# A two-layer hybrid decoder trunk on one core: the fifth Strassen product gets its own PSUM bank, and the turned tiles land in 1 KB rows

## The chip, the cores and the metric

The kernel runs on one core of one Trainium2 chip. The metric is the device time of one execution in microseconds (us), the median of three runs. Lower is better.

## The reference, cut to what matters

Two layers work on 256 rows of 2048 channels, all in float32. Each layer normalises its input, multiplies it with one wide weight matrix (`w_in`, 7680 columns), runs sliding-window attention and a spatial gating unit on parts of the product, projects both branches, merges them with sigmoid gates, multiplies with `w_out`, and adds the residual. Then comes a SwiGLU block with 5632 hidden channels.

```
for l in range(DEPTH):                       # DEPTH = 2, x: (1, 256, 2048) float32
    h = rms_norm(x, mix_norm[l])
    q, k, v, uv, gate_logits = jnp.split(h @ w_in[l], cuts, axis=-1)
...
    branch_a = sliding_window_attention(q, k, v, sinks[l]) @ w_attn_branch[l]
    branch_b = chunked_sgu(jax.nn.gelu(uv), w_spatial[l], b_spatial[l],
                           sgu_ln_g[l], sgu_ln_b[l]) @ w_sgu_branch[l]
    gates = jax.nn.sigmoid(gate_logits)
    merged = gates[..., :D_MODEL] * branch_a + gates[..., D_MODEL:] * branch_b
    x = x + merged @ w_out[l]
    h2 = rms_norm(x, ffn_norm[l])
    x = x + (jax.nn.silu(h2 @ w_gate[l]) * (h2 @ w_up[l])) @ w_down[l]
```

## The kernel before, in words

Everything is a list of **jobs**. A job multiplies the 256 rows with 1024 columns of a weight matrix (two column halves, c = 0 and c = 1, of 512 each; t = 0 and t = 1 are the two halves of the rows). The inner dimension is cut into **units** of 512 channels. To keep float32 accuracy each operand is split into a high part and a low part that TensorE (PE) takes as `fp32r`, and each product is three matmuls, `three` (L343 to L346): high by high, high by low, low by high.

A weight tile of 256 channels by 512 columns is a **part**. For each part SyncE loads raw weights (`raw`, four buffers of 1 MB), ScalarE (ACT) rounds them into `whi` (L224, six buffers), and VectorE (DVE) subtracts to get `wlo` (L232, five buffers). `Stream.fill` prepares parts some five ahead of PE: `whi` of part n + 6 and `wlo` of part n + 5 can be written once PE is done with part n.

In a "whole" step PE does 12 matmuls: one part with the two row halves. In 42 of the jobs (those with `m=1`, here called Strassen jobs) the first unit is done by Winograd's form of Strassen's algorithm instead: seven products of six matmuls each in place of four whole steps. The products are called 11, t1, t2, 22, t3, 21, t4; four of them need sums of weights, which DVE makes (L216, tiles `sum` and `raw`), and sums of the activations (`sh`, `sl`). The sum for t4 is the last of these four. The accumulators are PSUM banks a, e, x, y, four out of five; the fifth is idle in such a job. After product 11 ACT copies bank a into x (L383); after t1 it copies bank e, the fifth product, to SBUF (`p5`, the tile that the profile calls p; L385 and L369); after t2 it copies a to SBUF (`u2`, tile u, L387); after t3 it copies a into y (L389). PE's next product on the same bank has to wait for the copy: 22 is added into e, so it waits for p; t3 is added into a, so it waits for u; t4 is added into y. After t4 DVE adds u into e (L391) and p into a (L392). Banks x and y are C11 and C12 (column half 0), e and a are C21 and C22 (column half 1). Then the other units follow as whole steps, first both halves of column half 0, then both of column half 1 (L131 to L134).

Evictions are queued by `evicting` (L275). Column half 0 is done two steps before the job ends. For column half 1 row half 0 is evicted at once, row half 1 and a follow-up `then` are put off: time is counted in slots, a whole step is one slot, a Strassen product half a slot; behind a job whose successor is a Strassen job they come `T1_LATE` = 3 and `THEN_LATE` = 4 slots later.

The follow-up turns a result of 256 rows by 512 channels into the next job's stationary operand (`transposed`, L476). DVE transposes blocks of 32 by 32 (`blk`, L438, two instructions), GpSimd (POOL) issues 16 DMAs of 32 KB from SBUF to SBUF (`gathered`, L443), each in rows of 32 elements at the destination, into the tile `tt`. Then ACT rounds `tt` to `uh` (L486) and DVE makes `ul` (L493) one slot later. The place at which these readers are queued is reckoned from `G_BUSY` = 3.5 and `G_LAND` = 1.5 slots. An up-projection of the SwiGLU block, `w_out`, the second branch, and the last `w_down` have such a follow-up; for the second branch it begins with a merge of two gate tiles (L1003).

The order on every engine is that of the program as it is written; each engine works through its own list and waits where data is missing.

Of the kernel before, what the change touches and what calls it, by code (L numbers as in the profile page):

```python
# [14 lines left out]
P = 128  # L15
# [22 lines left out]
G_BUSY, G_LAND = 3.5, 1.5  # L38
T1_LATE, THEN_LATE = 3, 4
# [11 lines left out]
def hybrid_trunk(ctx: ExitStack, tc: tile.TileContext, x, mix_norm, w_in, q_norm, k_norm, sinks,  # L51
# [37 lines left out]
    PRODUCTS = ("11", "t1", "t2", "22", "t3", "21", "t4")  # L89
# [18 lines left out]
    def add_job(cols, units=None, m=0):  # L108
# [239 lines left out]
    def run(units, done):  # L348
# [3 lines left out]
        held = {}  # L352
# [13 lines left out]

        def kept(name, src):
            held[name] = temp(name=name)
            nc.scalar.activation(held[name], src, AF.Copy)  # L369

        for n, (name, u, at) in enumerate(job.steps):
# [3 lines left out]
            if name != "whole":  # L375
# [5 lines left out]
                if at:  # L381
                    if name == "11":
                        nc.scalar.activation(x, a, AF.Copy)  # L383
                    elif name == "t1":
                        kept("p5", e)  # L385
                    elif name == "t2":
                        kept("u2", a)  # L387
                    elif name == "t3":
                        nc.scalar.activation(y, a, AF.Copy)  # L389
                    elif name == "t4":  # L390
                        nc.vector.tensor_tensor(out=e, in0=e, in1=held["u2"], op=ALU.add)  # L391
                        nc.vector.tensor_tensor(out=a, in0=a, in1=held["p5"], op=ALU.add)  # L392
# [41 lines left out]
    def gathered(dst, src):  # L434
# [5 lines left out]
        ov = dst.rearrange("p k (t i c) -> p i (k t) c", t=NT, c=B)  # L440
        for i in range(4):
            for j in range(4):
                nc.gpsimd.dma_start(ov[j * B:(j + 1) * B, i],  # L443
                                  blk[i * B:(i + 1) * B, j].rearrange("p k t c -> p (k t) c"))
        gather_end[0] = max(gather_end[0], slot_no[0]) + G_BUSY
        return gather_end[0] + G_LAND - slot_no[0]

    def combine(unit, f, n, then=None):

        s4 = slot([P, 4, 2, P], name="sums")  # L450
        a11, a12, a21, a22 = (f[:, 2 * h:2 * h + 2, t * P:(t + 1) * P] for t in range(2) for h in range(2))

        def low(hi, lo, full):
            nc.vector.tensor_tensor(out=flat(lo), in0=flat(full), in1=flat(hi.bitcast(F32)), op=ALU.subtract)

        def first():
            for i, (p, q, op) in enumerate(((a21, a22, ALU.add), (s4[:, 0], a11, ALU.subtract),
                                            (a11, a21, ALU.subtract), (a12, s4[:, 1], ALU.subtract))):
                nc.vector.tensor_tensor(out=s4[:, i], in0=p, in1=q, op=op)
            if then is not None:  # L460
                nc.scalar.activation(unit.hi, f, AF.Copy)

        def second():
            if then is not None:
                low(unit.hi, unit.lo, f)
            nc.scalar.activation(unit.shi, s4, AF.Copy)

        def third():
            low(unit.shi, unit.slo, s4)
# [6 lines left out]
    def transposed(units, c, src, scale=None, cols=None, on_pe=False, sums=False, at_once=False):  # L476
# [3 lines left out]
        def scaled(k):  # L480
            return (scale or 1.0) if cols is None else cols[:, k:k + 1]
# [40 lines left out]
        tt = slot([P, 4, S], name="tt")  # L522
        n = gathered(tt, src)
        if not sums:
            after(n, lambda: highs(0, 4, tt))
            after(n + 1, lambda: (lows(0, 2, tt[:, 0:2]), lows(2, 2, tt[:, 2:4]), ready()))
            return

        def scale_all():
            if cols is not None or scale is not None:  # L530
                for k in range(4) if cols is not None else (None,):
                    kk = slice(0, 4) if k is None else slice(k, k + 1)
                    nc.scalar.activation(tt[:, kk], tt[:, kk], AF.Copy, scale=scaled(k))

        after(n, scale_all)
        combine(unit, tt, n + 1, ready)

    class Norm:
# [7 lines left out]
        def add_sums(self, c):  # L546
# [5 lines left out]
            combine(unit, f, 1)  # L552
# [49 lines left out]
    nc.gpsimd.dma_start(cs, cosine.rearrange("(t p) h -> p t h", p=P))  # L602
    nc.gpsimd.dma_start(sn, sine.rearrange("(t p) h -> p t h", p=P))
# [4 lines left out]
    nc.gpsimd.dma_start(vrows[:NB, :], mix_norm.rearrange("l (k p) -> (l k) p", p=P))  # L608
    nc.gpsimd.dma_start(vrows[NB:2 * NB, :], ffn_norm.rearrange("l (k p) -> (l k) p", p=P))
    nc.gpsimd.dma_start(vrows[2 * NB:, :], b_spatial.rearrange("l g i -> (l g) i"))  # L610
# [13 lines left out]
    after(11, columns)  # L624
# [3 lines left out]
    class Layer:  # L628


        def __init__(self, l):
            self.l = l
            self.wr = [None] * 2
            self.gn = lay.tile([P, 2, HD], F32, tag="gn", name=f"gn{l}")
            bcast(self.gn[:, 0, :], q_norm[l])
# [456 lines left out]
```

## Time and profile before

| what | value |
|---|---|
| median of three runs | 2511.05 us (2508.38 to 2511.25) |
| profiled execution | 2510.52 us |
| its span, first to last instruction | 2508.7 us |
| mean granted TensorE clock | 0.998 |
| PE busy (matmuls) | 2475.6 us, 99% |
| VectorE busy | 1907.1 us, 76% |
| ScalarE busy | 1343.6 us, 54% |
| GpSimd busy | 544.8 us, 22% |
| read from HBM | 475.27 MB |

The profile lists for each engine its instructions by line, with the tile that is written and the tiles that are read. "Idle before" is the time that the engine sat idle just before an instruction, and the name behind the arrow is what ended that wait. Matmuls are pipelined, so their own durations overlap; the distance from one start to the next is the cost. PEld is the load of the weights of a matmul (here the activations), which goes ahead of it.

### The profile page before, as it was taken

What the parts mean: (1) busy time and instruction counts of PE and PEld (TensorE: products, weight loads), DVE (VectorE), ACT (ScalarE), POOL (GpSimd) and SP (SyncE); (2) the same over time, 40 slices, a digit from 0 to 9 for tenths busy, and PEclk for the clock granted to TensorE, in tenths of its full rate; (3) what the DMA queues carried; (4) which work ended last, traced back from release to release, by engine and by line L of the source; (5) the groups of instructions that cost most, each with busy time, mean ns of one, the idle gap of its engine ahead of it and who ended that gap; (6) DMA issues with size and microseconds to landing.
All of it is one profiled execution on the core that took longest, in us unless ns stands there. A gap on an engine that the chain in (4) does not pass through costs nothing. (4 is left out here: it accounts for less than half of the span.)

```text
span 2508.7 us, 30665 instructions
## 1 busy us (share of the span) xinstructions
PE 2475.6 (99%) x11030; PEld 2021.6 (81%) x11030; DVE 1907.1 (76%) x2193; ACT 1343.6 (54%) x1652; POOL 544.8 (22%) x911
## 2 busy tenths in 40 slices
PE   9999999999999999999999999999999999999999
PEld 7888887788887888888888888877788788888877
DVE  6796667797877787777878956678878776868686
ACT  5455455465554555454654544554656455645554
POOL 1512202241220022003235122023402200220020
PEclk9999999999999999999999999999999999999999
DMA  7654656566565656656576446565756655665664
GB/s 270 217 171 158 211 196 200 192 203 220 198 217 185 231 189 214 206 201 213 189 255 217 163 157 216 192 198 184 231 204 222 210 200 208 195 224 178 210 188 164
DMA packets 161880, 507.71 MB, mean 202 GB/s; under 512 B 22016, under 2 KB 24672, under 8 KB 161728
## 3 DMA queue, kind: packets, MB, share of 16 engines
q1 hardware_dynamic: 133408, 476.87, 56.6%
q0 software_dynamic: 28000, 28.62, 4.4%
q8 instruction: 86, 1.41, 0.2%
q14 instruction: 66, 0.54, 0.1%
q10 hardware_dynamic: 320, 0.27, 0.0%
HBM read 475.27 MB, written 2.10 MB: 190 GB/s over the span
## 5 line engine op out<-in xcount | busy, mean ns | idle before, releaser
L232 DVE TENSOR_TENSOR wlo<-raw,whi 128x1024 fp32r<-128x1024 f32 (+1 forms) x940 | 1134.0, 1217 | 447.4 <-PE acc L345 345.8
L224 ACT ACTIVATE whi<-raw 128x1024 fp32r<-128x1024 f32 (+1 forms) x940 | 975.9, 1056 | 769.5 <-PE acc L346 647.5
L344 PE MATMUL acc<-whi,uh 128*128 128x512 f32 x3164 | 1242.2, 393 | 7.5 <-ACT uh L486 5.5
L345 PE MATMUL acc<-wlo,uh 128*128 128x512 f32 x3164 | 1233.6, 390 | 3.0 <-DVE wlo L232 3.0
L346 PE MATMUL acc<-whi,ul 128*128 128x512 f32 x3164 | 1234.3, 390 | 0.0
L443 POOL DMA_DIRECT2D tt<-blk x768 | 442.5, 584 | 1673.4 <-DVE blk L438 975.4
L344 PEld LDWEIGHTS acc<-whi,uh 128*128 128x128 f32 x3164 | 595.1, 188 | 139.2 <-ACT uh L486 7.8
L346 PEld LDWEIGHTS acc<-whi,ul 128*128 128x128 f32 x3164 | 594.9, 188 | 127.6 <-DVE ul L493 2.6
L345 PEld LDWEIGHTS acc<-wlo,uh 128*128 128x128 f32 x3164 | 595.2, 188 | 125.9 <-DVE wlo L232 4.3
L344 PE MATMUL acc<-whi,sh 128*128 128x512 f32 x336 | 137.7, 410 | 16.1 <-ACT p L369 16.1
L224 ACT ACTIVATE whi<-sum 128x1024 fp32r<-128x1024 f32 x84 | 89.2, 1062 | 107.3 <-DVE sum L216 60.8
L346 PE MATMUL acc<-whi,sl 128*128 128x512 f32 x336 | 131.5, 391 | 0.0
L345 PE MATMUL acc<-wlo,sh 128*128 128x512 f32 x336 | 131.3, 391 | 0.0
L232 DVE TENSOR_TENSOR wlo<-sum,whi 128x1024 fp32r<-128x1024 f32 x84 | 102.4, 1220 | 6.5 <-PE acc L345 6.5
L344 PEld LDWEIGHTS acc<-whi,sh 128*128 128x128 f32 x336 | 62.9, 187 | 50.7 <-ACT p L369 31.7
L493 DVE SCALAR_TENSOR_TENSOR ul<-tt,uh 128x512 fp32r<-128x512 f32 x56 | 36.2, 687 | 67.0 <-ACT uh L486 61.9
L486 ACT ACTIVATE uh<-tt 128x1024 fp32r<-128x1024 f32 x28 | 29.6, 1058 | 93.1 <-DMA tt<-blk 87.7
L346 PEld LDWEIGHTS acc<-whi,sl 128*128 128x128 f32 x336 | 63.1, 188 | 14.0
L345 PEld LDWEIGHTS acc<-wlo,sh 128*128 128x128 f32 x336 | 63.2, 188 | 10.3
L216 DVE TENSOR_TENSOR raw<-raw,sum 128x1024 f32<-128x1024 f32 x42 | 51.4, 1224 | 1.4
L216 DVE TENSOR_TENSOR raw<-raw,raw 128x1024 f32<-128x1024 f32 x42 | 51.2, 1219 | 0.0
L216 DVE TENSOR_TENSOR sum<-raw 128x1024 f32<-128x1024 f32 x42 | 51.2, 1219 | 0.0
(140 smaller groups left out, 1118.8 us busy)
## 6 DMA issues: line engine op xcount, KB each, us to landing
raw<-in_w_in_dram SPq DMA_DIRECT2D x112, 1024.0 KB, 5.2
raw<-in_w_down_dram SPq DMA_DIRECT2D x88, 1024.0 KB, 6.3
raw<-in_w_gate_dram SPq DMA_DIRECT2D x80, 1024.0 KB, 5.5
raw<-in_w_up_dram SPq DMA_DIRECT2D x80, 1024.0 KB, 5.2
raw<-in_w_out_dram SPq DMA_DIRECT2D x32, 1024.0 KB, 6.7
tt<-blk POOLq DMA_DIRECT2D x768, 32.0 KB, 5.0
raw<-in_w_attn_branch_dram SPq DMA_DIRECT2D x16, 1024.0 KB, 6.2
raw<-in_w_sgu_branch_dram SPq DMA_DIRECT2D x16, 1024.0 KB, 5.6
```

The source lines that it names most:

```text
L216: nc.vector.tensor_tensor(out=self.raw(dst), in0=self.raw(total[0]), in1=self.raw(total[1]), op=ALU.subtract)
L224: nc.scalar.activation(hi[:, k, :], raw[:, k, :], AF.Copy)
L232: nc.vector.tensor_tensor(out=lo[:, k, :], in0=raw[:, k, :], in1=hi[:, k, :].bitcast(F32), op=ALU.subtract)
L344: nc.tensor.matmul(ps, a, hi, start=first, stop=False, skip_group_check=True)
L345: nc.tensor.matmul(ps, a, lo, start=False, stop=False, skip_group_check=True)
L346: nc.tensor.matmul(ps, b, hi, start=False, stop=last, skip_group_check=True)
L443: nc.gpsimd.dma_start(ov[j * B:(j + 1) * B, i], blk[i * B:(i + 1) * B, j].rearrange("p k t c -> p (k t) c"))
L486: nc.scalar.activation(unit.hi[:, k0 + k:k0 + k + step, :], src_t[:, k:k + step, :], AF.Copy, scale=scaled(k0 + k))
L493: nc.vector.scalar_tensor_tensor(out=flat(unit.lo[:, kk, :]), in0=flat(src_t[:, k:k + step, :]), scalar=scaled(k0 + k), in1=flat(unit.hi[: ...
```

## The change

There are five edits.

1. A Strassen job takes all five banks. The fifth product has a bank q of its own, and the order of the products becomes 11, t1, t2, 21, t3, 22, t4. After t2 ACT copies a into e, and product 22 is added into e. The copy of the fifth product to SBUF comes after product 21 and is read by DVE's two adds at the end alone; both adds take the same tile. Four copies stay four copies.
2. In units that aren't a job's last, the whole steps go by channel half first and by column half second. So the first whole step after t4 still writes x and y, and the second one already writes e and a.
3. The block transposes' DMAs write rows of 1 KB (32 rows of 256 elements) into a tile with the axes block, unit, row half, column; the readers on ACT and DVE pick the order with their access pattern. Attention's query tile keeps the old form. The norms' column scales, four ACT instructions, are applied in place before one rounding; the factor 0.5 in front of `w_out` moves into the residual's eviction.
4. The numbers: `T1_LATE` 3 to 1.5, `THEN_LATE` 4 to 3, `G_LAND` 1.5 to 2.2.
5. Eight small loads at the start (rotary tables, norm vectors, sinks) are issued 2 and 3 slots later, and two steps that read them one slot later.

```diff
-G_BUSY, G_LAND = 3.5, 1.5
-T1_LATE, THEN_LATE = 3, 4
+G_BUSY, G_LAND = 3.5, 2.2
+T1_LATE, THEN_LATE = 1.5, 3
...
-    PRODUCTS = ("11", "t1", "t2", "22", "t3", "21", "t4")
+    PRODUCTS = ("11", "t1", "t2", "21", "t3", "22", "t4")
...
-                for c in range(2):
-                    for h in range(2):
-                        parts.append(((ab[h], c), None, ab[h]))
-                        job.steps.append(("whole", u, (h, c)))
+                order = [(h, c) for h in range(2) for c in range(2)]
+                if u == job.units[-1]:
+                    order = [(h, c) for c in range(2) for h in range(2)]
+                for h, c in order:
+                    parts.append(((ab[h], c), None, ab[h]))
+                    job.steps.append(("whole", u, (h, c)))
...
-        n = 4 if job.pair else 2
+        n = 5 if job.m else 4 if job.pair else 2
...
-            a, e, x, y = own
+            a, q, x, e, y = own
             ps = [[x, y], [e, a]]
-            banks[:] = [banks[4], banks[2], banks[3], banks[1], banks[0]]
-            into = {"11": a, "t1": e, "t2": a, "22": e, "t3": a, "21": x, "t4": y}
-            begun = {id(x), id(y)}
+            banks[:] = [banks[1], banks[2], banks[4], banks[3], banks[0]]
+            into = {"11": a, "t1": q, "t2": a, "22": e, "t3": a, "21": x, "t4": y}
+            begun = {id(x), id(y), id(e)}
...
-                    if name == "11":
-                        nc.scalar.activation(x, a, AF.Copy)
-                    elif name == "t1":
-                        kept("p5", e)
-                    elif name == "t2":
-                        kept("u2", a)
-                    elif name == "t3":
-                        nc.scalar.activation(y, a, AF.Copy)
+                    if name in ("11", "t2", "t3"):
+                        nc.scalar.activation({"11": x, "t2": e, "t3": y}[name], a, AF.Copy)
+                    elif name == "21":
+                        fifth = temp(name="p5")
+                        nc.scalar.activation(fifth, q, AF.Copy)
                     elif name == "t4":
-                        nc.vector.tensor_tensor(out=e, in0=e, in1=held["u2"], op=ALU.add)
-                        nc.vector.tensor_tensor(out=a, in0=a, in1=held["p5"], op=ALU.add)
+                        for d in (e, a):
+                            nc.vector.tensor_tensor(out=d, in0=d, in1=fifth, op=ALU.add)
...
-        ov = dst.rearrange("p k (t i c) -> p i (k t) c", t=NT, c=B)
         for i in range(4):
             for j in range(4):
-                nc.gpsimd.dma_start(ov[j * B:(j + 1) * B, i],
-                                  blk[i * B:(i + 1) * B, j].rearrange("p k t c -> p (k t) c"))
+                src = blk[i * B:(i + 1) * B, j].rearrange("p k t c -> p (k t) c")
+                d = dst[j * B:(j + 1) * B]
+                nc.gpsimd.dma_start(blocks(d)[:, :, i] if whole else d[:, i].rearrange("p k t c -> p (k t) c"), src)
...
+        tv = tt.rearrange("p i k t c -> p (k t) i c")
...
+        def split():
+            scale_all()
+            nc.scalar.activation(blocks(unit.hi), tv, AF.Copy)
+
+        def lower():
+            nc.vector.tensor_tensor(out=blocks(unit.lo), in0=tv, in1=blocks(unit.hi).bitcast(F32), op=ALU.subtract)
+            ready()
...
-                                     self.kT[j * HD:(j + 1) * HD, g, :nk], start=True, stop=True)
+                                     self.kT[j * HD:(j + 1) * HD, :, g, :t + 1].rearrange("p i t c -> p t i c"), start=True, stop=True)
...
+    after(3, vectors)
+    after(12, columns)
```

**ACT, first `w_out` job of layer 0, from the copy after product 11 to the copy after t3.** Before (`p` is the fifth product's SBUF tile, `u` that of t2, `acc` are PSUM banks, `whi` the rounded weights; `whi<-sum` is the one for t4):

```order
L383 ACTIVATE acc_3339<-acc_3337 128x512
L224 ACTIVATE whi_3354<-sum_3227 128x1024
L369 ACTIVATE p_612_3364<-acc_3338 128x512
L224 ACTIVATE whi_3366<-raw_3209 128x1024
L369 ACTIVATE u_617_3380<-acc_3337 128x512
L224 ACTIVATE whi_3382<-raw_3229 128x1024
L224 ACTIVATE whi_3392<-raw_3209 128x1024
L389 ACTIVATE acc_3340<-acc_3337 128x512
```

and now, at the same place:

```order
L380 ACTIVATE acc_3335<-acc_3333 128x512
L226 ACTIVATE whi_3351<-sum_3223 128x1024
L226 ACTIVATE whi_3361<-raw_3205 128x1024
L380 ACTIVATE acc_3336<-acc_3333 128x512
L226 ACTIVATE whi_3377<-raw_3205 128x1024
L383 ACTIVATE p_619_3387<-acc_3334 128x512
L226 ACTIVATE whi_3389<-raw_3225 128x1024
L380 ACTIVATE acc_3337<-acc_3333 128x512
```

The copy that stood directly behind `whi<-sum` is gone from there; the copy of t2 (into acc_3336, bank e) stands in the place that u had, behind two roundings, and the fifth product's copy stands one rounding later still.

**DVE, the same job, from the low part of t4's weights on.** Before (`gate` at L997 is the eviction of row half 1 of the job before, L1003 the merge, `blk` the block transposes, the two `acc` rows the adds at the end of the Strassen part):

```order
L232 TENSOR_TENSOR wlo_3368<-sum_3227,whi_3354 128x1024
L232 TENSOR_TENSOR wlo_3384<-raw_3209,whi_3366 128x1024
L232 TENSOR_TENSOR wlo_3394<-raw_3229,whi_3382 128x1024
L232 TENSOR_TENSOR wlo_3405<-raw_3209,whi_3392 128x1024
L997 SCALAR_TENSOR_TENSOR gate_3166<-gate_3166,acc_3172 128x512
L232 TENSOR_TENSOR wlo_3418<-raw_3229,whi_3403 128x1024
L391 TENSOR_TENSOR acc_3338<-acc_3338,u_617_3380 128x512
L392 TENSOR_TENSOR acc_3337<-acc_3337,p_612_3364 128x512
L232 TENSOR_TENSOR wlo_3432<-raw_3370,whi_3416 128x1024
L1003 TENSOR_TENSOR gate_2165<-gate_2165,gate_3166 128x1024
L438 STREAM_TRANSPOSE blk_3451<-gate_2165 128x4x4x32 x2
```

and now:

```order
L234 TENSOR_TENSOR wlo_3363<-sum_3223,whi_3351 128x1024
L1018 SCALAR_TENSOR_TENSOR gate_3162<-gate_3162,acc_3168 128x512
L234 TENSOR_TENSOR wlo_3379<-raw_3205,whi_3361 128x1024
L234 TENSOR_TENSOR wlo_3391<-raw_3205,whi_3377 128x1024
L234 TENSOR_TENSOR wlo_3404<-raw_3225,whi_3389 128x1024
L1024 TENSOR_TENSOR gate_2164<-gate_2164,gate_3162 128x1024
L432 STREAM_TRANSPOSE blk_3416<-gate_2164 128x4x4x32 x2
L234 TENSOR_TENSOR wlo_3437<-raw_3225,whi_3402 128x1024
L386 TENSOR_TENSOR acc_3336<-acc_3336,p_619_3387 128x512
L386 TENSOR_TENSOR acc_3333<-acc_3333,p_619_3387 128x512
L234 TENSOR_TENSOR wlo_3451<-raw_3365,whi_3435 128x1024
```

The eviction of row half 1 moved ahead by three rows, and the merge and the block transposes moved from behind the two adds to a place ahead of them. Where the job before has a follow-up without a merge, the block transposes alone moved so.

More of the change, by code (lines that the diff above doesn't have):

```diff
@@ L520, in transposed, with scale_all @@
             return
-        tt = slot([P, 4, S], name="tt")
+        tt = landed()
         n = gathered(tt, src)
-        if not sums:
[L525 to L536, printed above, removed]
+        tv = tt.rearrange("p i k t c -> p (k t) i c")
+        def scale_all():
+            if cols is not None:
+                for k in range(4):
+                    nc.scalar.activation(tt[:, :, k], tt[:, :, k], AF.Copy, scale=scaled(k))
+        def split():
[4 more added lines that the diff above has]
+            ready()
+        if not sums:
+            after(n, split)
+            after(n + 1, lower)
+        else:
+            after(n, scale_all)
+            combine(unit, tv, n + 1, ready)
     class Norm:
@@ L918, in mix, with residual @@
             after(1, gated)
-    def residual(units, nxt, sums, out_at=None):
+    def residual(units, nxt, sums, out_at=None, scale=None):
         for j in range(0, NCH, 2):
@@ L939, in added @@
                     sl = slice(o * CW + i * w, o * CW + (i + 1) * w)
-                    nc.vector.tensor_tensor(out=xs[:, t, sl], in0=ps[t][:, i * w:(i + 1) * w], in1=xs[:, t, sl],
-                                            op=ALU.add)
+                    src = ps[t][:, i * w:(i + 1) * w]
+                    if scale is None:
+                        nc.vector.tensor_tensor(out=xs[:, t, sl], in0=src, in1=xs[:, t, sl], op=ALU.add)
+                    else:
+                        nc.vector.scalar_tensor_tensor(out=xs[:, t, sl], in0=src, scalar=scale, in1=xs[:, t, sl],
+                                                       op0=ALU.mult, op1=ALU.add)
                     if out_at is not None:
@@ L1014, in hybrid_trunk @@
         norm = Norm(ffn_cols(l))
-        residual(mT, norm, M_FFN)
+        residual(mT, norm, M_FFN, scale=0.5)
         nxt = Norm(mix_cols(l + 1)) if l + 1 < DEPTH else None
```

58 lines of the change are left out of this document (31 added, 27 removed).

## The prediction

> **What bounds the kernel now.** I read the page first, then PE's waits and the weight loads' waits, then the timeline around them.
>
> ```profile
> span 2508.7 us, 30665 instructions
> PE 2475.6 (99%) x11030; PEld 2021.6 (81%) x11030; DVE 1907.1 (76%) x2193; ACT 1343.6 (54%) x1652; POOL 544.8 (22%) x911
> ...
> PE acc L344 <- ACT p L369: 16.1, 27, 1.6
> PE acc L344 <- ACT uh L486: 5.5, 5, 3.2
> ...
> PEld acc L344 <- ACT p L369: 31.7, 42, 2.0
> PEld acc L344 <- ACT uh L486: 7.8, 6, 3.7
> ```
>
> TensorE is busy for 99% of the span, and no edit removes a matmul. What can be won is its waiting: the copy of the fifth product (p), in all 42 Strassen jobs, and late stationary operands (uh). Everything else is far off PE's path.
>
> How such a wait comes about, in one job whose predecessor is an up-projection:
>
> ```profile
> 1883.70 0.39 PE L344 MATMUL acc<-whi,sh 128*128 128x512 f32 x1
> ...
> 1886.20 0.39 PE L346 MATMUL acc<-whi,sl 128*128 128x512 f32 x1
> 1886.91 0.50 PE L344 MATMUL acc<-whi,sh 128*128 128x512 f32 x1 [0.32 <-ACT p L369]
> ...
> 1892.56 0.39 PE L344 MATMUL acc<-whi,uh 128*128 128x512 f32 x1
> ```
> ```profile
> 1884.00 1.22 DVE L216 TENSOR_TENSOR sum<-raw,raw 128x1024 f32<-128x1024 f32 x1
> 1885.31 1.06 ACT L224 ACTIVATE whi<-sum 128x1024 fp32r<-128x1024 f32 x1 [0.83 <-DVE sum L216]
> 1886.28 0.57 ACT L369 ACTIVATE p<-acc 128x512 f32<-128x512 f32 x1
> 1886.75 1.05 ACT L224 ACTIVATE whi<-raw 128x1024 fp32r<-128x1024 f32 x1
> 1887.70 0.59 ACT L369 ACTIVATE u<-acc 128x512 f32<-128x512 f32 x1
> ```
>
> From 1883.70 (t1) to 1886.20 are eleven intervals, 0.227 us each; six make a product, 1.36 us. Product 22 was due at T = 1886.43 and came at 1886.91. The copy p was late because ACT stood at `whi<-sum`, and that waited for DVE's sum, which began at 1884.00. So DVE, behind on its list, is late first. From t1 to the first whole step at 1892.56 are 36 matmuls, 8.16 us unhindered; they took 8.86. I call the 0.70 the job's loss; it holds the wait and the slow restart behind it.
>
> **The change part by part.** *Own bank.* Each of the 42 jobs has its loss read in this way. There are four kinds; one job of each of the other three:
>
> ```profile
> 1926.56 0.39 PE L344 MATMUL acc<-whi,sh 128*128 128x512 f32 x1
> 1935.20 0.39 PE L344 MATMUL acc<-whi,uh 128*128 128x512 f32 x1
> ...
> 2013.23 0.39 PE L344 MATMUL acc<-whi,sh 128*128 128x512 f32 x1
> 2022.01 0.39 PE L344 MATMUL acc<-whi,uh 128*128 128x512 f32 x1
> ...
> 462.82 0.39 PE L344 MATMUL acc<-whi,sh 128*128 128x512 f32 x1
> 472.95 0.39 PE L344 MATMUL acc<-whi,uh 128*128 128x512 f32 x1
> ```
>
> Kind A (15 jobs, first pair: 0.48; 0.21 to 0.48, in sum 5.3): DVE's sum was in time and the wait is a matter of the hand-over. Kind B (8 jobs, second pair: 0.62; in sum 6.8): the sum is late, no follow-up comes behind. Kind C (15 jobs, the one at 1883.70; in sum 11.9): as B, and block transposes follow. Kind D (4 jobs, third pair: 1.97; in sum 7.9): as C with a merge. Together 31.9, against the 31.7 of the weight loads' row.
>
> Removing the wait for p doesn't remove ACT's lateness. PE's next need of ACT is now the copy of t2, due at T + 1.36, and it stands behind `whi<-sum` and one more rounding. By the rows above a rounding takes 0.95 to 0.97 of ACT's time, so this copy begins at 1885.31 + 0.97 + 0.95 = 1887.23, ends at 1887.82, and t3, due at 1887.79, starts at about 1887.88. The copy into y sits behind two roundings and one copy more; the same steps give some 0.15. Kind A has 0.4 to spare at t3 and keeps 0.1 a job, 1.5 in sum: **-3.8**. Kind B keeps ACT's lateness: its loss was the start of `whi<-sum` + 1.60 - T (here 0.48) and becomes, at the copy into y, that start + 1.36 - T; with a restart of 0.2 each that is 4.4 in sum, **-2.4**.
>
> *Follow-up ahead of the adds.* In C and D the follow-up now stands on DVE before the two adds, and by the new order of halves bank e is wanted one whole step (2.72 us) after t4, not two. DVE's rows of the C job:
>
> ```profile
> 1880.55 1.29 DVE L438 STREAM_TRANSPOSE blk<-hid 128x512 f32<-128x512 f32 x2
> ...
> 1891.55 0.75 DVE L1037 SCALAR_TENSOR_TENSOR hid<-acc,rr,hid 128x512 f32<-128x512 f32 x1
> 1892.21 1.21 DVE L232 TENSOR_TENSOR wlo<-raw,whi 128x1024 fp32r<-128x1024 f32 x1
> 1893.35 0.69 DVE L391 TENSOR_TENSOR acc<-acc,u 128x512 f32<-128x512 f32 x1
> ```
>
> DVE runs without a gap into the add at 1893.35. Two transposes (1.21) ahead of it put it at 1894.56, done by 1895.25 and seen by PE at 1895.31. PE wants bank e at T + 4 products + one step = 1886.43 + 5.44 + 2.72 = 1894.59. Loss 0.72 plus a restart of 0.2: 0.92 in place of 0.70, so 15 x 0.22 = **+3.3**. What ACT costs at t3 and y is hidden in it. A kind D job:
>
> ```profile
> 468.38 3.63 DVE L232 TENSOR_TENSOR wlo<-raw,whi 128x1024 fp32r<-128x1024 f32 x3
> ...
> 473.65 0.69 DVE L391 TENSOR_TENSOR acc<-acc,u 128x512 f32<-128x512 f32 x1
> ...
> 475.99 1.22 DVE L1003 TENSOR_TENSOR gate<-gate,gate 128x1024 f32<-128x1024 f32 x1
> 477.24 1.30 DVE L438 STREAM_TRANSPOSE blk<-gate 128x512 f32<-128x512 f32 x2
> ```
>
> T is 462.82 + 2.72 = 465.54. The add moves by 1.25 + 1.22 to 476.12, seen at 476.87; wanted at 465.54 + 8.16 = 473.70. Loss 3.17 + 0.16 against 1.97: 4 x 1.36 = **+5.4**. The bounds: nothing, if DVE makes up the 0.7 (C) beforehand; double, if the restart costs what the longest wait below shows.
>
> *Late operands.* The longest of the uh waits is in the first `w_out` job:
>
> ```profile
> 494.49 0.39 PE L346 MATMUL acc<-whi,ul 128*128 128x512 f32 x1
> 498.11 0.50 PE L344 MATMUL acc<-whi,uh 128*128 128x512 f32 x1 [3.24 <-ACT uh L486]
> ...
> 499.68 0.63 PE L346 MATMUL acc<-whi,ul 128*128 128x512 f32 x1
> ...
> 503.30 0.40 PE L346 MATMUL acc<-whi,ul 128*128 128x512 f32 x1
> ```
> ```profile
> 479.12 1.16 POOL L443 DMA_DIRECT2D tt<-blk  x2 [5.13 <-PE acc L346]
> 481.41 6.33 POOL L443 DMA_DIRECT2D tt<-blk  x11 [1.13 <-issue]
> 489.92 0.58 POOL L443 DMA_DIRECT2D tt<-blk  x1 [2.18 <-DMA tt<-blk]
> 491.55 1.16 POOL L443 DMA_DIRECT2D tt<-blk  x2 [1.05 <-DMA tt<-blk]
> ...
> 497.00 1.06 ACT L486 ACTIVATE uh<-tt 128x1024 fp32r<-128x1024 f32 x1 [9.19 <-DMA tt<-blk]
> ```
>
> From 494.49 to 503.30 are 15 matmuls, 3.40 us; they took 8.81, so 5.4 lost. The other five waits are 7.8 - 3.7 = 4.1, with some 0.2 of restart each 5.0. This is a chain from the block transposes to landing, rounding and PE. The merge now follows the three low parts that begin at 468.38 (3.63, of which the next hides 0.09) and one eviction (0.60 of DVE's time), so at 472.52 in place of 475.99: 3.47 us sooner, with its DMAs behind it. The operand is then ready at 494.64, and PE, itself 1.36 later, wants it at 496.08. The other five are late by under 1.0 us and come 3.5 sooner too. A seventh gain of 0.5 is an eviction of the last `w_down`, held up behind a late uh. All of it goes: **-10.9**; down to -5.5 if only the long one does.
>
> The Trainium skill speaks against the 1 KB rows (DMA: Bandwidth & Descriptors, "Why small descriptors are slow (HBM only)"): transfers from SBUF to SBUF don't suffer from small pieces. On the rows above, POOL's gaps of 2.18 and 1.05 for landings say that something does hold up these DMAs. By the skill the sum stays at -10.9 with 1.4 us to spare; by the rows it has up to 4 more. That is why the operand's rival below keeps a chance.
>
> *The rest.* Reading and writing in runs of 32 elements: a row of such runs, and one without, both of 512 elements:
>
> ```profile
> L940 DVE TENSOR_TENSOR xs<-acc,xs 128x512 f32<-128x512 f32 x62 | 41.0, 682 | 6.4 <-PE acc L346 6.4
> ...
> L728 DVE TENSOR_TENSOR sq<-q,sa 128x512 f32<-128x512 f32 x8 | 5.1, 682 | 0.0
> ```
>
> No difference, so I price it, the scale in the residual's eviction, and the score matmuls' new pattern at nothing, covered by idle ACT and DVE outside the Strassen parts. The later small loads could give or take 0.5 at the start; I take nothing.
>
> Sum: -3.8 - 2.4 + 3.3 + 5.4 - 10.9 = -8.4 us. The profiled execution took 2510.5, 1.8 more than its span and 0.5 under the median, so 2502.1 on its scale and **2502.5 us** as a median.
>
> **The rivals.** *ACT and DVE catch up*, so that neither the copy of t2 nor the adds hold PE: for it, PE's idle time is small and DVE is busy for 76% only; against it, DVE has no gap in the rows above. Half of 31.9 gone gives 2510.5 - 16 - 10.9 = 2484, all of it 2468. *A wash*: operands stay late where POOL's queue or the later readers (`G_LAND`) hold them, so that only half of the 10.9 comes, and the adds cost the 8.7 as priced plus a restart of 0.2 more in 19 jobs: 2510.5 - 6.2 + 8.7 + 3.8 - 5.5 = 2511. *Slower: the strided readers are slow*, a mechanism of its own. With the reader queued later, DVE makes the low part of the job's third unit right behind the `wlo` that PE sets free one step ahead; from there PE wants it after a step and two matmuls, 3.17 us. Hand-over 0.1, that `wlo` 1.14 (1892.21 to 1893.35) and the reader of the same size 1.22 leave 0.6 to spare, and as much at the fourth unit. If runs of 32 cost twice (1.22 more), PE waits 0.6 + 0.4 at two units in each of eight jobs (of each layer the first `w_out` job, the first gate job, and the first `w_down` job of two rounds), 16 us, with the rest as forecast: 2502.1 + 16 = 2518. It decides from 1.5 times the duration on; the row at L728 speaks against it.
>
> A further rule: the Trainium skill (TensorE: Matmul & The Clock Gate, "A second HAM failure mode: psum-queue depth-cycling") says that many short idle times can throw the clock to half. Here the 42 waits did not: after 1886.91 the whole stretch lost only 0.70. After the long wait the nine matmuls from 499.68 to 503.30 took 3.62 in place of 2.04, so 1.6 lost; at all 19 adds that were 30 us, 2532.
>
> **How the numbers follow.** Forecast 0.55, with 2498 to 2507 as its own range; catching up 0.15; wash 0.20; strided readers 0.08; clock 0.02. The range 2493 to 2512 leaves out most of catching up and the slower pair, about 2 in 10. A difference of 0.2% (5 us) is about what a measurement of this kernel can tell from none: faster are the forecast but for its upper end and catching up, 0.68; same 0.23; slower 0.09.
>
> **What would show it.** Right: no PE wait for p; the weight loads wait for the copy into e by 0.1 in C jobs and over 1 in D jobs; a new PE wait for DVE's add at the second whole step, 0.7 in 15 jobs and near 1.7 on top in four; no wait for uh over 0.5. Wrong: 36 matmuls from t1 in 8.2 us in C jobs, no wait for the adds, or `uh` rounding over 1.3 us.

## The result, and the profile after

| what | before | after |
|---|---|---|
| median, same chip | 2509.72 us (2506.95 to 2511.25) | 2487.78 us (2486.52 to 2489.2) |
| profiled execution, span | 2508.7 us | 2484.8 us |
| mean granted TensorE clock | 0.998 | 0.999 |

The ratio is 0.9914 with a 95% interval of 0.9897 to 0.9931: 21.9 us faster, where 8.4 had been forecast and the range ended at 2493. The changed kernel's page and the waits of PE and of its weight loads (in total, times, longest):

```profile
span 2484.8 us, 30610 instructions
PE 2464.7 (99%) x11030; PEld 2023.1 (81%) x11030; DVE 1901.5 (77%) x2135; ACT 1359.2 (55%) x1660; POOL 479.5 (19%) x911
...
PE acc L346 <- ACT acc L380: 5.0, 4, 1.4
PE acc L346 <- DVE acc L386: 4.6, 4, 1.2
...
PEld acc L346 <- ACT acc L380: 18.1, 48, 1.9
PEld acc L346 <- DVE acc L386: 13.1, 19, 1.6
```

The waits for p and for uh are gone. In their place stand waits for the copies into a bank (L380) and for DVE's adds (L386), 19 of the latter, as many as there are C and D jobs. Here is a C job (t1 at 1866.68, second whole step at 1878.18) and a D job (t1 at 461.23, t3 at 466.64, second whole step at 475.12) on PE:

```profile
1866.68 0.39 PE L346 MATMUL acc<-whi,sh 128*128 128x512 f32 x1
...
1878.18 0.50 PE L346 MATMUL acc<-whi,uh 128*128 128x512 f32 x1
1878.51 0.40 PE L347 MATMUL acc<-wlo,uh 128*128 128x512 f32 x1
...
461.23 0.39 PE L346 MATMUL acc<-whi,sh 128*128 128x512 f32 x1
...
466.64 0.50 PE L346 MATMUL acc<-whi,sh 128*128 128x512 f32 x1 [1.17 <-ACT acc L380]
...
475.12 0.50 PE L346 MATMUL acc<-whi,uh 128*128 128x512 f32 x1 [1.21 <-DVE acc L386]
```

and DVE in the same C job, the transposes ahead of the add as the order had shown:

```profile
1875.11 1.29 DVE L432 STREAM_TRANSPOSE blk<-hid 128x512 f32<-128x512 f32 x2
1876.33 1.18 DVE L234 TENSOR_TENSOR wlo<-raw,whi 128x1024 fp32r<-128x1024 f32 x1
1877.43 1.28 DVE L386 TENSOR_TENSOR acc<-acc,p 128x512 f32<-128x512 f32 x2
```

The add begins 10.75 after t1; the prediction had 10.86. Bank e was due 48 matmuls after t1, at 1877.56, and came 0.62 late; the first interval after it is 0.33 in place of 0.227, so a restart costs some 0.1 here. The job's whole excess is 0.75, where 0.92 was forecast.

Kinds A and B are another matter. A B job, before (first pair of matmuls: t1 and the first whole step) and the rows of ACT and DVE ahead of it:

```profile
1840.21 0.39 PE L344 MATMUL acc<-whi,sh 128*128 128x512 f32 x1
...
1849.70 0.39 PE L344 MATMUL acc<-whi,uh 128*128 128x512 f32 x1
```
```profile
1826.50 1.71 ACT L486 ACTIVATE uh<-tt,vcols 128x256 fp32r<-128x256 f32 x4 [5.43 <-DMA tt<-blk]
...
1842.22 1.06 ACT L224 ACTIVATE whi<-sum 128x1024 fp32r<-128x1024 f32 x1 [1.23 <-DVE sum L216]
```
```profile
1827.05 1.69 DVE L493 SCALAR_TENSOR_TENSOR ul<-tt,vcols,uh 128x256 fp32r<-128x256 f32 x4 [1.75 <-ACT uh L486]
...
1840.91 1.22 DVE L216 TENSOR_TENSOR sum<-raw,raw 128x1024 f32<-128x1024 f32 x1
```

ACT stood for 5.43 us at a rounding whose data had not landed, and DVE behind it; from there DVE had no gap wider than 0.46 up to the fourth sum, 14 us later, at 1840.91. That is where most of the 1.33 of this job (9.49 - 8.16) came from: with the readers alone moved, in a run below, it loses 0.46. The same job after the change, on PE and on DVE:

```profile
1824.49 0.39 PE L346 MATMUL acc<-whi,sh 128*128 128x512 f32 x1
...
1832.68 0.39 PE L346 MATMUL acc<-whi,uh 128*128 128x512 f32 x1
```
```profile
1817.73 1.22 DVE L234 TENSOR_TENSOR wlo<-raw,whi 128x1024 fp32r<-128x1024 f32 x1 [0.70 <-PE acc L347]
...
1823.17 1.23 DVE L234 TENSOR_TENSOR wlo<-raw,whi 128x1024 fp32r<-128x1024 f32 x1 [0.75 <-PE acc L347]
1824.31 1.22 DVE L218 TENSOR_TENSOR sum<-raw,raw 128x1024 f32<-128x1024 f32 x1
```

DVE now waits for PE (0.70, 0.75): it has caught up. The sum begins 0.18 before t1, not 0.70 behind it, and the loss is 0.03. How long ACT sat idle for landings before these roundings, in the groups by line, before:

```profile
L486 ACT ACTIVATE uh<-tt 128x1024 fp32r<-128x1024 f32 x28 | 29.6, 1058 | 93.1 <-DMA tt<-blk 87.7 <-DMA gn<-in_k_norm_dram 5.4
L486 ACT ACTIVATE uh<-tt,vcols 128x256 fp32r<-128x256 f32 x40 | 17.1, 499 | 41.7 <-DMA tt<-blk 41.7
L461 ACT ACTIVATE uh<-tt 128x1024 fp32r<-128x1024 f32 x10 | 10.6, 1055 | 8.1 <-DMA tt<-blk 7.5 <-issue 0.5
```

and after:

```profile
L535 ACT ACTIVATE uh<-tt 128x1024 fp32r<-128x1024 f32 x38 | 40.3, 1059 | 34.6 <-DMA tt<-blk 32.5 <-DMA gn<-in_k_norm_dram 1.7
L531 ACT ACTIVATE tt<-tt,vcols 128x256 f32<-128x256 f32 x48 | 20.5, 497 | 11.3 <-DMA tt<-blk 11.3
L464 ACT ACTIVATE uh<-tt 128x1024 fp32r<-128x1024 f32 x10 | 10.5, 1046 | 1.7 <-DMA tt<-blk 1.7
```

136.9 us have become 45.5. The readers themselves take what they took (1058 and 1059 ns). The experiments ask whether that is what ended the losses of kinds A and B, or the bank.

### The profile page after: what moved, and what is told of

Read it like the earlier page. It is cut to its first block, busy times and chain, and to the rows that moved or that the text cites. A ratio compares the mean times of both kernels' runs of the same rounds, so it can differ in the third digit from the quotient of the medians.

```text
span 2484.8 us, 30610 instructions
## 1 busy us (share of the span) xinstructions
PE 2464.7 (99%) x11030; PEld 2023.1 (81%) x11030; DVE 1901.5 (77%) x2135; ACT 1359.2 (55%) x1660; POOL 479.5 (19%) x911
## 5 line engine op out<-in xcount | busy, mean ns | idle before, releaser
L438 POOL DMA_DIRECT2D tt<-blk x800 | 393.1, 498 | 1721.8 <-DVE blk L432 1042.6
L346 PE MATMUL acc<-whi,sh 128*128 128x512 f32 x336 | 132.7, 395 | 5.0 <-ACT acc L380 5.0
L380 ACT ACTIVATE acc<-acc 128x512 f32<-128x512 f32 x126 | 73.7, 585 | 10.0 <-PE acc L348 10.0
L538 DVE TENSOR_TENSOR ul<-tt,uh 128x1024 fp32r<-128x1024 f32 x38 | 46.4, 1222 | 17.9 <-ACT uh L535 16.1
L535 ACT ACTIVATE uh<-tt 128x1024 fp32r<-128x1024 f32 x38 | 40.3, 1059 | 34.6 <-DMA tt<-blk 32.5
L386 DVE TENSOR_TENSOR acc<-acc,p 128x512 f32<-128x512 f32 x84 | 54.1, 689 | 0.0
```

What stands on the lines that cost most here:

```text
L346: nc.tensor.matmul(ps, a, hi, start=first, stop=False, skip_group_check=True)
L380: nc.scalar.activation({"11": x, "t2": e, "t3": y}[name], a, AF.Copy)
L386: nc.vector.tensor_tensor(out=d, in0=d, in1=fifth, op=ALU.add)
L438: nc.gpsimd.dma_start(blocks(d)[:, :, i] if whole else d[:, i].rearrange("p k t c -> p (k t) c"), src)
L535: nc.scalar.activation(blocks(unit.hi), tv, AF.Copy)
L538: nc.vector.tensor_tensor(out=blocks(unit.lo), in0=tv, in1=blocks(unit.hi).bitcast(F32), op=ALU.subtract)
```

## The experiments

Theory 1: readers that stand in ACT's and DVE's lists ahead of their landing hold both engines up, so that the sums are late; where they are placed is worth as much as the bank. Theory 2: the new bank and order of copies free PE by themselves. The runs come in three groups of four, each with its own runs of the kernel before on the same chip: 2509.96 for the first four, 2509.78 for the next, 2510.09 for the last. "Loss" is again the time over 8.16 from t1 to the first whole step after t4.

**The bank alone**, in the kernel before.

```diff
-    PRODUCTS = ("11", "t1", "t2", "22", "t3", "21", "t4")
+    PRODUCTS = ("11", "t1", "t2", "21", "t3", "22", "t4")
...
-            a, e, x, y = own
+            a, q, x, e, y = own
...
```

> The kernel before with the own bank and the new order of products alone (edit 1); halves, rows, numbers and small loads as before. Before is 2509.7 us. Theory 1 (what made ACT late in kinds B and C was DVE's and ACT's readers of gathers that had not landed; this edit doesn't touch them, so ACT's lateness stays and passes on to the copies for t3 and t4): A 15 jobs -5, B -2.4, C -4.5, D -0.6 each, no uh wait gone: about 2496 to 2499, and B jobs still lose 0.4 or more between t1 and the first whole step. Theory 2 (the new order of copies frees PE whatever ACT's lateness is): 36 matmuls from t1 in 8.2 us in A, B and C: -24 to -28, so 2482 to 2486, the B jobs lose under 0.1. In both there is no PE wait for p and uh waits stay near 5.5.

Measured: 2594.98 us, ratio 1.0335 (1.0321 to 1.0349), 85 us slower; both theories missed. PE's waits, then ACT and DVE in one job:

```profile
PE acc L344 <- ACT acc L378: 88.6, 49, 2.5
```
```profile
663.59 0.58 ACT L378 ACTIVATE acc<-acc 128x512 f32<-128x512 f32 x1 [2.10 <-DVE hid L1029]
```
```profile
662.75 0.75 DVE L1029 SCALAR_TENSOR_TENSOR hid<-acc,rr,hid 128x512 f32<-128x512 f32 x1
```

The copy into y waits for DVE's eviction of the job before: with five banks in use there is none left over, and y is still full, since `T1_LATE` = 3 queues that eviction three slots behind. In most jobs this costs 2.0 to 2.6 at t4. So the bank and `T1_LATE` = 1.5 are one edit; the prediction had treated the numbers as moving the follow-up alone.

**The bank undone**, the other four edits in.

```diff
-    PRODUCTS = ("11", "t1", "t2", "21", "t3", "22", "t4")
+    PRODUCTS = ("11", "t1", "t2", "22", "t3", "21", "t4")
...
```

> The changed kernel with edit 1 undone: fifth product in SBUF and the old order of products, the other four edits in. Changed is 2487.8 us. Theory 1 (readers no longer hold ACT and DVE, so the sums are in time): the wait for p stays but at the hand-over's size of kind A, 0.3 to 0.4 in each of 42 jobs, kind B falls from 0.85 to 0.4: 2487.8 + 42 x 0.35 = 2502. Theory 2 (the readers have nothing to do with it): the jobs lose what they lost before, 31.9, against 14.0 in the changed kernel: 2487.8 + 18 = 2506, B jobs at 0.85.

Measured: 2495.04 us, 0.9940 (0.9926 to 0.9953): 7.3 slower than the changed kernel. B jobs lose 0.24 to 0.35 (the two with eight transposes of PE inside the stretch 1.1, 0.9 of it those), against 0.6 to 1.4 before. The sums are in time without the bank, as theory 1 has it: in all eight B jobs the fourth sum's rounding begins 1.46 us or more before T, the start due to the product behind t2. It expected 2502, since it charged C and D with the wait for p too; there the wait for the adds comes behind it and swallows it: over their whole jobs kinds C and D lose 23.2, with the own bank 22.7. The bank earns in A and B alone, 6.0.

**The halves undone** in the changed kernel: column half first in every unit.

```diff
-                order = [(h, c) for h in range(2) for c in range(2)]
-                if u == job.units[-1]:
-                    order = [(h, c) for c in range(2) for h in range(2)]
-                for h, c in order:
-                    parts.append(((ab[h], c), None, ab[h]))
-                    job.steps.append(("whole", u, (h, c)))
+                for c in range(2):
+                    for h in range(2):
+                        parts.append(((ab[h], c), None, ab[h]))
+                        job.steps.append(("whole", u, (h, c)))
```

> The changed kernel with edit 2 undone: whole steps of every unit go by column half first, so bank e is wanted two whole steps after t4 instead of one. The trace of the changed kernel has 19 waits for DVE's adds, longest 1.38, lost time 8.15 us in sum. Theory 1 and 2 alike: all 19 go, 2487.8 - 8 = 2480. Rival: the raw weights of the second channel half are held longer or wanted in another order, and weight parts come late: 2488 or more, with new PE waits for whi or wlo.

Measured: 2477.54 us, 0.9870 (0.9857 to 0.9884), 10.2 faster than the changed kernel. All 19 waits for the adds are gone, and over their whole jobs kinds C and D lose 12.0 in place of 22.7. No wait for weights is new; what stays is the copies and the waits for weights at the very start, which the kernel before has too:

```profile
PE acc L344 <- ACT acc L378: 4.7, 4, 1.2
PE acc L345 <- DVE wlo L232: 2.8, 2, 2.5
PE acc L344 <- ACT whi L224: 1.7, 1, 1.7
```

**The numbers undone** in the changed kernel.

```diff
-G_BUSY, G_LAND = 3.5, 2.2
-T1_LATE, THEN_LATE = 1.5, 3
+G_BUSY, G_LAND = 3.5, 1.5
+T1_LATE, THEN_LATE = 3, 4
```

> The changed kernel with the numbers 3, 4 and 1.5 of before (edit 4 undone): follow-ups come behind the adds again, their DMAs start about 3.5 us later, their readers are queued 0.7 slots sooner behind them. Theory 1: readers stall ACT and DVE again, sums are late in kind B jobs (0.3 or more each between t1 and the first whole step) and most of the uh waits are back, +5 to +8; the 19 add waits (8.15) go: 2485 to 2491 with both effects visible in the trace. Theory 2: the B jobs stay under 0.1, the uh waits come back (+5), the add waits go (-8): 2484 to 2486.

Measured: 2580.83 us, 1.0284 (1.0270 to 1.0298). It is the first run's wait again (88.1 us of PE for the copy into y), so it tells nothing of the readers. The next four runs take the numbers apart.

**The bank with `T1_LATE`**, in the kernel before.

```diff
-T1_LATE, THEN_LATE = 3, 4
+T1_LATE, THEN_LATE = 1.5, 4
...
-    PRODUCTS = ("11", "t1", "t2", "22", "t3", "21", "t4")
+    PRODUCTS = ("11", "t1", "t2", "21", "t3", "22", "t4")
...
```

> The kernel before with the own bank, the new order of products and T1_LATE 1.5 in place of 3 (the row half left over is evicted earlier); the rest as before, so halves in the old order, late readers and late operands. Before is 2510.0. From the run with the own bank alone: there t4 waited 2.0 to 2.6 in each of 42 jobs for ACT's copy into y, which stood behind the late eviction of that bank; T1_LATE 1.5 should take that away whole. Theory 1 (the readers' stalls make ACT late in kinds B, and that stays here): A 15 jobs lose under 0.05 each (5.3 gone), B loses what is left of its lateness at the copies for t3 and t4 (start of the fourth sum's rounding + 1.36 after the due time), 2.8 in sum (4.0 gone), C 0.4 each (6 gone), D 1.65 each (1.3 gone), uh waits stay: 2510 - 16.5 = 2493.5. Theory 2 (the bank alone frees everything): 2510 - 24 = 2486.

Measured: 2502.10 us, 0.9970 (0.9958 to 0.9981), 7.7 faster; the copy into y no longer holds t4 for 2 us, so the 85 us of the first run were the late eviction. Kind A loses 0.8 in sum (5.3 before), 0.5 of it in one job, D 6.5 (7.9): nearly as expected. B loses 5.1 and C 10.5, more than expected by 2.3 and 4.5, and theory 2 is out. ACT still sits idle for landings:

```profile
L478 ACT ACTIVATE uh<-tt 128x1024 fp32r<-128x1024 f32 x28 | 29.6, 1058 | 96.7 <-DMA tt<-blk 90.9 <-DMA gn<-in_k_norm_dram 5.8
L478 ACT ACTIVATE uh<-tt,vcols 128x256 fp32r<-128x256 f32 x40 | 17.1, 498 | 46.2 <-DMA tt<-blk 46.2
```

With the third group as above that is 141 us against 136.9. A sooner PE meets landings that are no sooner, so some of its sums are later: in the B job shown above the rounding of the fourth sum begins 0.06 before T, in the kernel before 0.71.

**The readers later, alone**: one number in the kernel before.

```diff
-G_BUSY, G_LAND = 3.5, 1.5
+G_BUSY, G_LAND = 3.5, 2.2
```

> The kernel before with G_LAND 2.2 in place of 1.5 alone: the readers of a gather stand 0.7 slots later in ACT's and DVE's lists, behind parts that PE needs sooner. Theory 1 (readers that wait for a landing hold up ACT and DVE, and so the sums): the fourth sum's rounding in B jobs starts 0.3 to 0.9 sooner, kind B falls from 6.8 to about 3, C's worst four from 4.4 to 2.4; the uh waits change little, being set by the landing: 2510 - 5 = 2505. Theory 2 (readers harmless): 2508 to 2511, B jobs unchanged at 0.6 to 1.4. Rival 3: the reader is now itself the late one and uh waits grow by 1 to 2 each: 2512 or more.

Measured: 2503.09 us, 0.9973 (0.9962 to 0.9985), 6.7 faster, where theory 1 had some 5. In all eight B jobs the fourth sum's rounding begins 1.58 before T (before: 0.42 to 1.20), ACT's idle time for landings is 43.5 in place of 136.9, and kind B falls from 6.8 to 2.2. The job shown above, on ACT:

```profile
1820.74 1.71 ACT L486 ACTIVATE uh<-tt,vcols 128x256 fp32r<-128x256 f32 x4 [0.60 <-DMA tt<-blk]
...
1838.91 1.06 ACT L224 ACTIVATE whi<-sum 128x1024 fp32r<-128x1024 f32 x1 [0.35 <-DVE sum L216]
```

0.60 of waiting in place of 5.43. Two PE waits for uh are left, 3.26 and 3.47 long. The first was 3.24 before, but the second was 0.61: the third theory's effect, in one place. A wait for ul (0.9) is new. The two waits of the attention for pT (0.9 lost each) and one of 1.0 in the first job of layer 1 are gone too; the prediction had only the last, at half of that.

**The rows alone**: edit 3 in the kernel before.

```diff
-                nc.gpsimd.dma_start(ov[j * B:(j + 1) * B, i],
-                                  blk[i * B:(i + 1) * B, j].rearrange("p k t c -> p (k t) c"))
+                src = blk[i * B:(i + 1) * B, j].rearrange("p k t c -> p (k t) c")
+                d = dst[j * B:(j + 1) * B]
+                nc.gpsimd.dma_start(blocks(d)[:, :, i] if whole else d[:, i].rearrange("p k t c -> p (k t) c"), src)
...
```

> The kernel before with edit 3 alone: 1 KB rows, one reader in place of four where there are column scales, the 0.5 in the eviction. The changed kernel's POOL issues took 498 ns in place of 584 a DMA, so sixteen of them end 1.4 sooner. Theory 1: operands land 1 to 2 us sooner, the uh waits shrink from 10.9 to about 5, B jobs gain some 2, the wait of the first attention's pT goes or stays: 2510 - 8 = 2502. Theory 2 (landing time rules, not issue): uh waits stay, 2508 to 2511. If the strided readers are slow, uh's rounding is over 1.3 us and the time is over 2512.

Measured: 2498.91 us, 0.9957 (0.9944 to 0.9969), 10.9 faster. PE's waits for uh fall from 5.5 to one of 0.4 (three for ul, 1.6 in sum, are new), B falls from 6.8 to 2.3, and ACT's idle time for landings is 104.7. The readers stand where they stood, but in all eight B jobs the fourth sum's rounding now begins 1.55 or more before T: in the B job shown above ACT's wait for the landing ends 16.0 us ahead of t1, in the kernel before 13.7. So a sooner landing does here what a later reader does. In one place the wait came back. A kind A job (t1 at 1914.22) lost 3.37 in place of 0.48, since DVE stood behind a reader and came to the fourth sum 2.7 us after t1:

```profile
1904.11 1.22 DVE L544 TENSOR_TENSOR ul<-tt,uh 128x1024 fp32r<-128x1024 f32 x1 [6.58 <-ACT uh L541]
...
1916.95 1.22 DVE L216 TENSOR_TENSOR sum<-raw,raw 128x1024 f32<-128x1024 f32 x1
```

POOL's issues, before and in this run (duration in ns, least, median, most):

```profile
L443 POOL DMA_DIRECT2D tt<-blk x768: 582/584/632, 201.8 to 2424.1; - x192
```
```profile
L444 POOL DMA_DIRECT2D tt<-blk x800: 496/496/567, 62.9 to 2410.6; - x160
```

**The follow-ups sooner, alone**, in the kernel before.

```diff
-T1_LATE, THEN_LATE = 3, 4
+T1_LATE, THEN_LATE = 1.5, 3
```

> The kernel before with T1_LATE 1.5 and THEN_LATE 3 alone: the follow-up stands ahead of DVE's two adds, its DMAs start about 3.5 us sooner, and bank e is still wanted two whole steps after t4. As worked out in the prediction, the late operands come 3.5 sooner: 10.9 gone, nothing lost at the adds: 2510 - 11 = 2499. Rival: ACT and DVE do the same work in a worse place (transposes ahead of the sums make p later by 1 us or more in the 19 jobs with a follow-up): 2505 or more.

Measured: 2501.61 us, 0.9971 (0.9962 to 0.9980), 8.2 faster. The PE waits for uh are gone, but B rises from 6.8 to 9.1 and C from 12.0 to 13.9: the readers are placed by the same count of slots, and so moved sooner with the transposes; ACT's idle time for landings rises from 136.9 to 156.9.

So each of these four takes its part of the late operands, sums or copies, 7.7, 6.7, 10.9 and 8.2 us. The parts overlap: the second and the third both bring B's sums in time, the third and the fourth both end the waits for uh (but for 0.4), and the first and the last share `T1_LATE`. The last four runs take the kernel with the halves undone (2477.54) as their mate, the run to compare with.

**The small loads undone as well.**

```diff
...
-    after(3, vectors)
-    after(12, columns)
+    after(11, columns)
...
```

> The changed kernel with edit 2 (halves) and edit 5 (small loads later) undone; its mate is the run with the halves alone undone, 2477.5. Profiled executions so far show the first job's excess anywhere from 7.7 to 10.6 us, with the small loads late or not. Both theories: edit 5 is worth nothing, 2476 to 2479. Rival: the late small loads do free the weights at the start, 2479 to 2481.

Measured: 2476.74 us, 0.9867 (0.9855 to 0.9880). Edit 5 is worth nothing that can be told. The first job's excess differs by up to 2.9 us between profiled executions, late loads or not.

**`G_LAND` undone as well.**

```diff
-G_BUSY, G_LAND = 3.5, 2.2
+G_BUSY, G_LAND = 3.5, 1.5
```

> The changed kernel with edit 2 undone and G_LAND back at 1.5 (readers 0.7 slots sooner); mate 2477.5. Theory 1 (readers ahead of their landing stall ACT and DVE): with rows of 1 KB and sooner follow-ups the data still land some 14 us after the transposes, so the readers stall again in part: the fourth sum is late again in some of the B jobs, 2480 to 2484. Theory 2 (rows and sooner follow-ups cover it alone): 2477 to 2478, B's sums stay at -1.46 to -1.59.

Measured: 2484.70 us, 0.9899 (0.9887 to 0.9912): 7.2 slower than its mate. Four of the eight B sums are later again (by 0.24 to 0.95), C loses 9.4 in place of 5.2, the attention's pT waits are back, and ACT's idle time for landings is 123.8 in place of 57.7. Theory 2 is out here too.

**`THEN_LATE` undone as well.**

```diff
-T1_LATE, THEN_LATE = 1.5, 3
+T1_LATE, THEN_LATE = 1.5, 4
```

> The changed kernel with edit 2 undone and THEN_LATE back at 4, T1_LATE 1.5: the follow-ups of the second column half come behind DVE's adds again; mate 2477.5. If sooner follow-ups still pay when the rows are 1 KB and the readers late: uh or ul waits come back in the w_out and first w_down jobs, 2479 to 2483. If rows and readers alone made the operands timely, 2477 to 2478.

Measured: 2482.20 us, 0.9888 (0.9875 to 0.9901): 4.7 slower, with waits for the low part in C and D jobs:

```profile
PE acc L346 <- DVE ul L536: 2.2, 8, 0.5
```

**The first half's follow-up later.**

```diff
-                after(1, then)
+                after(behind(1, 2.5), then)
```

> The changed kernel with edit 2 undone and the follow-up of the first column half moved from 1 to 2.5 slots behind when a Strassen job follows, so that merge and block transposes stand behind the fourth sum on DVE. The mate, 2477.5, still loses 1.65 in each of four D jobs and 0.25 to 0.41 in 15 C jobs, since ACT waits for that sum ahead of the copies: 6.6 + 5.3 = 11.9. Theory 1: the sums are in time as in kind A, all but 1 to 2 of the 11.9 goes, 2466 to 2468. Rival: the two follow-ups' DMAs now follow each other on POOL, the operands land later and uh waits come back: 2472 or more.

Measured: 2517.41 us, 1.0033 (1.0021 to 1.0045). This run's theory holds for the sums, and its rival decides the time. In ten C jobs and the four D jobs the rounding of the fourth sum began 1.11 before T and 0.15 behind it, in the kernel before and after the change alike (one D job 0.42), so moving the readers did nothing there; what delays it is the first half's follow-up. Here it begins 1.58 ahead in all fourteen, and the ten C jobs lose 0.02 or less. But the operands come late:

```profile
PE acc L344 <- ACT uh L533: 16.1, 8, 2.4
PE acc L344 <- ACT acc L378: 8.3, 14, 1.8
PE acc L346 <- DVE ul L536: 7.4, 16, 0.9
```

A step that is moved out of one chain's way is moved into another's.

## Why the prediction was wrong

The terms, in us, from the two profiled executions (time over 0.2267 per matmul, job by job; the uh waits that lie in C and D jobs stand with the operands):

| term | forecast | measured |
|---|---|---|
| kind A | -3.8 | -5.1 |
| kind B | -2.4 | -6.7 |
| kind C with the adds | +3.3 | -1.9 |
| kind D with the adds | +5.4 | +4.7 |
| late operands | -10.9 | -11.4 |
| the rest | 0 | -3.5 |
| sum | -8.4 | -23.9 |

**Right.** The waits for p go. The follow-up stands ahead of the adds, bank e is wanted a step sooner, and 19 new waits come of it: D within 0.2 a job of its price, C within 0.2 in ten of its 15 jobs. The halves cost 10.2 by experiment. The late operands were sized rightly, though the prediction had them go by the sooner follow-up alone, and the rows do nearly the same without it; the strided readers cost nothing, as the row at L728 had said (1058 against 1059 ns). The clock stayed at 0.999.

**The step that failed** is "Kind B keeps ACT's lateness". It took the late sum as given, as if DVE's load made it late, and carried it over into the new kernel. But in kind B and in three C jobs "DVE, behind on its list" was behind because of the readers, 14 us up the list, that wait for landings; these were being moved by edits 3 and 4 at the same time, and the prediction priced them for PE's wait on uh alone. With G_LAND alone kind B fell from 6.8 to 2.2, with the rows alone to 2.3. This is 4.3 in kind B. It also lowers the base from which C was reckoned. Ten of its 15 jobs lose 0.75, but in the other five the fourth sum is now rounded 1.24 ahead of time, and they lose some 0.5. That is 3.5 less than forecast, 3.0 of it in three jobs whose sum was late before: they had lost 0.95 to 1.85, to which the prediction added 0.22.

**A second step**, "with a restart of 0.2 each", was mis-sized. In the C job that the prediction shows, 0.70 is 0.48 of lateness and a first interval of 0.33, which is 0.1 over; the last 0.1 is spread over the intervals up to the next product, whose weight loads waited for the copy u as well (8.6 us in 42 jobs). That last part is a second hand-over, not a restart. In the trace after, A loses 0.02 a job in place of 0.1, and in C bank e came 0.62 late in place of 0.72, with a restart of 0.1 in place of 0.2. Over A, C and D that is 1.3 + 1.7 + 0.7.

**A third**, "The rest" at zero, missed 1.8 from the attention's two waits, which belong to the same readers (they go with `G_LAND` alone, and return when it alone is undone). The other 1.6, at the start, is the scatter of profiled executions, not edit 5; it is part of why the spans differ by 23.9 and the medians by 21.9.

Of the rivals, "ACT and DVE catch up" came nearest (2484 with half of the loss gone), but by its number more than its mechanism: the sums caught up, while the adds do hold PE, 19 times. And "against it, DVE has no gap in the rows above" was too little to hold it at 0.15: those rows are of one job and a few us, and in a kind B job a view that short begins after the stall that had used the gap up. The three steps make 4.3 + 3.5 + 3.7 + 3.5 = 15.0 of the 15.5 between forecast and trace; 0.5 more is the operands.

One dependence was not seen at all, though it changed nothing in the sum: the bank needs the earlier eviction, and without it costs 85 us. And one term was right but its consequence was not drawn: if the new order of halves costs what the C and D terms say, the kernel without it is faster, and it is, by 10.2.

## What to carry to other kernels

An engine that is "behind" at the place where PE waits is to be followed up its list to the last place where it sat idle for something else than work: that wait, here a reader queued ahead of its landing 14 us before, was the cause in the B jobs, and an edit that moves it can pay everywhere behind it. Edits that share a clock or a pool of buffers (a bank and the eviction that empties it, a gather and its readers) are priced together, since one of them alone can be a loss of 85 us. Where one part of a change has a price of its own in the sum, the kernel without that part is worth a run: 2477.5, and 2476.7 with the small loads left alone too, against 2487.8.

## What the runs showed of the hardware

A DMA from SBUF to SBUF whose destination has rows of 1 KB took POOL 496 to 498 ns to issue, with rows of 32 elements 584; sixteen of them end 1.4 us sooner. The transfer itself was shorter too. POOL's queue moved the same packets and bytes in every run, nearly all of the bytes these DMAs; here is the time that its packets took as a share of 16 DMA engines' span, in the kernel before and with the rows alone:

```profile
q0 software_dynamic: 28000, 28.62, 4.4%
...
q0 software_dynamic: 28000, 28.62, 3.9%
```

All runs with the old rows have 4.3 or 4.4 there, all with the new rows 3.8 or 3.9. The Trainium skill (DMA: Bandwidth & Descriptors, "Why small descriptors are slow (HBM only)") holds small pieces harmless between SBUF and SBUF; the prediction gave both that and the landing gaps, and kept its sum. By the run with the rows alone (10.9 us faster, ACT's waiting for landings from 136.9 to 104.7) and by the queue's share, the traces here speak against taking that rule as the whole cost. How much of the 10.9 is the issue, how much the transfer, and how much the single reader in place of four, was not taken apart.

The rival of a falling clock did not come: the granted clock is 1.00 from 100 to 2470 us after the change, with the waits for the adds, 1.2 us at most on PE. The 1.6 us that the prediction read behind the longest wait were such a fall, though. From 500 to 504 us the clock granted in the kernel before was 0.62, and with the readers later alone it was 0.59 over the four us behind each of the waits of 3.26 and 3.47. With the bank alone, which has 49 waits of up to 2.5 for the copies, the mean clock was 0.991.
